# Two transformer layers on one core: read-back copies kept in order on VectorE, query and key splits cut map by map, and another order behind layer 0's last projection

## The chip, the cores and the metric

The kernel runs on one core of a Trainium2 chip. The metric is the device time of one execution in microseconds (us). A page of the profile and the trace come from one further execution, taken by the hardware profiler. The engines are named as there: PE is TensorE, PEld its weight loads, DVE VectorE, ACT ScalarE, POOL GpSimd and SP SyncE, which here mainly issues DMAs. All data in the tables and rows below is fp32 or fp32r, with the tiles named by the program (`Q`, `E`, `M` and so on; a letter behind a `P`, as in `PC`, is a bank of PSUM).

## The reference, cut to what matters

Layer 0 mixes tokens by differential attention, layer 1 by attention over a neighbourhood of the latent grid plus the context. Each is followed by an MLP with a squared ReLU. Shift, scale and gate of every normalization ("modulation") come from a matrix product of a conditioning vector.

```python
D_MODEL, SEQ, CTX_LEN, HEAD_DIM, DEPTH = 1024, 512, 256, 64, 2
DA_HEADS, NA_HEADS, D_FF = 8, 16, 4096

def diff_attend(q, k, v, lam):                 # two maps (m) per head
    s = jnp.einsum('bqhmd,bkhmd->bhmqk', q, k) * ATTN_SCALE
    p = jax.nn.softmax(s, axis=-1)
    w = p[:, :, 0] - lam * p[:, :, 1]
    return jnp.einsum('bhqk,bkhe->bqhe', w, v)

for i in range(DEPTH):
    mod_l = jnp.split(jax.nn.silu(c) @ w_mod[i] + b_mod[i], 6, axis=-1)
    mod_c = jnp.split(jax.nn.silu(c_ctx) @ w_mod[i] + b_mod[i], 6, axis=-1)
    h_l = rms_norm(x, norm1_g[i]) * (1 + mod_l[1]) + mod_l[0]
    h_c = rms_norm(ctx, norm1_g[i]) * (1 + mod_c[1]) + mod_c[0]
    y_l, y_c = mixer[i](h_l, h_c)              # q and k: rms_norm per map, rotary in layer 0
    x = x + mod_l[2] * y_l
    x = x + mod_l[5] * mlp(rms_norm(x, norm2_g[i]) * (1 + mod_l[4]) + mod_l[3])
    # layer 0 does the same for ctx with mod_c
return x
```

Matrix products are needed at fp32 accuracy.

## The kernel before, in words

**Data and stages.** There are 768 tokens: 256 of the context and 512 latent ones, 6 tiles of 128 rows. A product at fp32 accuracy is made of three passes over operands that are each split into a high part (rounded to fp32r) and the remainder, low part (`PASSES`); so most tiles are written twice, the high part by an ACT copy and the low part by a subtraction on DVE. In the profile the stages lie about so: layer 0's first head to 65 us, its heads to 421, its last attention and the projection of heads to 563, its MLP to 1057, layer 1's eight groups of two heads from 1091 to 1403, their projection to 1476, the last MLP to the end.

**The order of the work.** In the attention stages the order is written out by hand in strings that `run()` reads word by word: `START0`, `CYCLE0` for each further head, `TURN0` and `END0` behind the last projection of layer 0's heads, and `START1`, `CYCLE1`, `LAST1`, `END1` for layer 1. A word is a step: Q a half of the projection of one tile to q, k and v; U a turn, which transposes and splits q and k of two tiles (U4 is the turn of tiles 4 and 5); S scores and softmax of one tile; T transposes and splits the softmax of one tile ("turned"); V weighs the values with it; O transposes one tile's output; P half a step of the projection of heads (P0a and P0b are the halves of step 0), x and X fetch and split one head's attention output for it, B begins it; w and c load and split the weights of the next head; m is a visit of the modulation. A prime marks the head before, two primes the one before that. In layer 1 U turns likewise, and N is a piece of a normalization. PE, SP and POOL issue in the written order (`manual_schedule(engines=PINNED)`); for DVE and ACT a scheduler sets the order, except for instructions that are given to `keep_in_program_order`.

**The visits.** The modulation's large product is spread over 40 loads of weights, one for each visit (class `Mods`, l. 1060). A visit runs 8 matmuls with a tile `M` of raw weights (l. 300; rows of the profile that group two visits show x16), adds them up in `MA` (l. 302) and issues the load of the next `M`. From layer 0's second head to the end of its projection there is one buffer for `M`. After the fourth visit of a section the result is stored to DRAM (`rows`). One visit later `rows` is read back into the tile `columns`, turned so that the model dimension lies on the partitions (the DMA is issued on SP). Again a visit later `mod_set` copies `columns` into `mB` (l. 287) or, with the norm's gain, into `mA` (l. 290). The program writes that copy at the visit behind the one that issues the read-back; on DVE the scheduler is free to put it anywhere behind the issue. There are six such copies in the profile.

**A turn.** In layer 0 four transposes (l. 522) put q and k of two tiles into one PSUM bank `C`: the columns 0 to 255 are q, 256 to 511 are k, and the partitions 0 to 63 and 64 to 127 belong to the two maps. `q_split` and `k_split` (l. 450 and 463) write them to SBUF so that each map's scores contract over 128 partitions: q's high part on its own half and the low part on the other and k's high and low parts on both halves each. Their lines are:

| line | engine | what it writes for map m, with a the map's own half and b the other |
|---|---|---|
| 456, 457 | ACT, DVE | layer 0's q: high part in half a, low part in half b |
| 459, 460 | ACT, DVE | the same for layer 1's q, with a gain |
| 467, 469 | ACT | k's high part in a, then in b, both from PSUM |
| 468, 471 | DVE | k's low part in a; for tiles 4 and 5 in b as well, from PSUM |
| 473 | POOL | k's low part in b for the other tiles, from the SBUF half a |

ACT and DVE read the same bank, and the program's waits let them in by turns. Layer 0's turn calls `q_split` first for tiles 0 to 3 and last for tiles 4 and 5 (l. 527 to 531). Layer 1 turns into a bank `A` (transposes l. 664, calls l. 667 to 669); its scores are l. 686, layer 0's are l. 547. Ahead of a turn, a projection (matmuls l. 431) is copied to SBUF (l. 438, ACT), squared there (l. 442, ACT), summed (l. 444, DVE) and scaled (l. 446, DVE), and the low part of the values is written (l. 492, DVE).

**Behind layer 0's last projection.** `TURN0` and `END0` finish the last two heads (weighing l. 582, turned softmax l. 571, output l. 599) and mix in the projection of heads (l. 783, followed by a multiply with the gate at l. 788 and an addition at l. 789, for which the layer's input is fetched by SP). Five visits lie in them.

## Time and profile before

| | |
|---|---|
| median of 3 timed runs | 1846.56 us (1844.48 to 1847.8) |
| profiled execution | 1841.2 us |
| its span | 1839.4 us |
| mean granted clock of PE | 0.977 of full speed |
| PE busy | 1722.8 us, 94% of the span, 9918 matmuls |
| PEld busy | 1519.8 us, 83% |
| DVE busy | 1253.5 us, 68% |
| ACT busy | 937.6 us, 51% |
| POOL busy | 1039.7 us, 57% |
| DMA | 227.29 MB, mean 124 GB/s |

How its rows are read: a row of an instruction has its start, its duration, engine, line, operation, the tiles out and in, and in brackets how long the engine stood idle just before and what ended that wait. A row "a:b" of the windows has the length of the stretch, then for PE, PEld, DVE, ACT and POOL the busy time with the number of instructions, then the mean granted clock of PE, the share of the DMA engines and the GB/s. A row that starts with a line number groups like instructions: busy time and mean ns of one, then the idle time before them by releaser. The line "DMA columns<-rows" is of the list of waits: the idle time that this DMA ended, and the number of times.

### The profile page before, as it was taken

How to read it: one execution, taken by the hardware profiler on the slowest of the kernel's cores; microseconds unless marked ns; L12 is line 12 of the kernel's file. 1: busy time of each engine (PE TensorE's matmuls, PEld its weight loads, DVE VectorE, ACT ScalarE, POOL GpSimd, SP SyncE). 2: the span in 40 equal slices, each digit the busy share in tenths (PEclk: the TensorE clock that was granted, in tenths of full speed). 3: DMA queues.
4: the chain of work that ended last, by engine and by line, in shares of the span. 5: the costliest groups of instructions: out<-in, count | busy, mean ns of one | idle time of the engine just before them, and what ended most of it. 6: DMA issues, size and time to landing. Idle time of an engine off the chain costs nothing.

```text
span 1839.4 us, 27551 instructions
## 1 busy us (share of the span) xinstructions
PE 1722.8 (94%) x9918; PEld 1519.8 (83%) x9918; DVE 1253.5 (68%) x2332; ACT 937.6 (51%) x1962; POOL 1039.7 (57%) x998
## 2 busy tenths in 40 slices
PE   6989999997899999999999999999998889999998
PEld 4878989985688899999997888889887778788877
DVE  4678878886565656464659677778677566676785
ACT  4566767765234343343333456667667254445432
POOL 3755666652334667575767713433355448777774
PEclk9989999998999999999999999999999989999999
DMA  9222221225445545544541334433332434334441
GB/s 335 73 84 78 91 83 64 93 79 190 155 152 165 166 124 146 136 121 100 154 143 58 106 127 130 132 109 118 107 119 96 145 103 138 126 126 138 137 149 46
DMA packets 104809, 227.29 MB, mean 124 GB/s; under 512 B 22160, under 2 KB 38752, under 8 KB 100576
## 3 DMA queue, kind: packets, MB, share of 16 engines
q1 hardware_dynamic: 95152, 212.56, 36.7%
q10 hardware_dynamic: 9520, 12.97, 2.0%
q8 instruction: 78, 1.28, 0.3%
q14 instruction: 59, 0.48, 0.1%
HBM read 207.19 MB, written 18.30 MB: 123 GB/s over the span
## 4 chain that ended last, share of the span: by engine, by line
PE 69%; DVE 12%; ACT 6%; DMA 5%; issue 4%; POOL 4%; ACTq 0%; SPq 0%; POOLq 0%; DVEq 0%
PE PD L875 21%; PE PA L431 14%; PE PA L935 8%; PE PB L935 8%; PE PA L783 3%; PE PA L1016 3%; POOL W L162 2%; PE PS L547 2%; PE PB L582 2%; PE PQ L421 1%; PE PS L686 1%; PE PB L732 1%; PE PB L717 1%; ACT E L553 1%; PE PB L571 1%
## 5 line engine op out<-in xcount | busy, mean ns | idle before, releaser
L162 POOL TENSOR_TENSOR W<-R,W 128x512 fp32r<-128x512 f32 x214 | 328.5, 1561 | 143.4 <-ACT W L156 142.0
L875 PE MATMUL PD<-Q,W 128*128 128x384 f32 (+2 forms) x1992 | 381.5, 345 | 7.2 <-DVE Q L352 6.0
L875 PEld LDWEIGHTS PD<-Q,W 128*128 128x128 f32 x1992 | 348.1, 190 | 30.2 <-DVE Q L352 7.3
L156 ACT ACTIVATE W<-R 128x1024 fp32r<-128x1024 f32 (+1 forms) x137 | 138.7, 1014 | 138.5 <-POOL W L162 34.9
L162 POOL TENSOR_TENSOR W<-N,W 128x512 fp32r<-128x512 f32 x98 | 141.8, 1469 | 114.7 <-ACT W L156 95.3
L935 PE MATMUL PA<-W,H 128*128 128x512 f32 x732 | 191.2, 396 | 6.5 <-DVE Q L943 3.1
L935 PE MATMUL PB<-W,H 128*128 128x512 f32 x738 | 191.2, 394 | 3.2 <-DVE Q L943 2.0
L431 PE MATMUL PA<-W,Q 128*128 128x384 f32 (+1 forms) x1008 | 175.2, 326 | 0.0
L935 PEld LDWEIGHTS PA<-W,H 128*128 128x128 f32 x732 | 138.9, 191 | 36.1 <-issue 3.5
L935 PEld LDWEIGHTS PB<-W,H 128*128 128x128 f32 x738 | 139.4, 190 | 32.9 <-DVE Q L943 2.7
L431 PEld LDWEIGHTS PA<-W,Q 128*128 128x128 f32 x1008 | 159.4, 192 | 1.0 <-ACT H L469 0.2
L312 POOL TENSOR_TENSOR SQ<-SQ,half 128x4 f32<-128x4 f32 (+1 forms) x96 | 94.0, 980 | 109.6 <-DVE SQ L444 108.2
L431 PE MATMUL PA<-WB,H 128*128 128x384 f32 x576 | 110.0, 343 | 4.8 <-DVE Q L492 4.8
L156 ACT ACTIVATE W<-N 128x1024 fp32r<-128x1024 f32 x49 | 51.8, 1058 | 113.4 <-PE PB L935 36.8
L431 PEld LDWEIGHTS PA<-WB,H 128*128 128x128 f32 x576 | 99.9, 190 | 6.2 <-DVE Q L492 3.9
L783 PE MATMUL PA<-W,H 128*128 128x512 f32 x384 | 98.5, 408 | 6.0 <-DVE T L788 5.3
L875 PE MATMUL PD<-H,W 128*128 128x512 f32 (+1 forms) x408 | 95.2, 382 | 0.2 <-DVE H L352 0.2
L783 PEld LDWEIGHTS PA<-W,H 128*128 128x128 f32 x384 | 72.7, 195 | 25.3 <-DVE T L788 6.4
L698 POOL TENSOR_SCALAR E<-E,SA 128x256 f32<-128x256 f32 x64 | 59.1, 935 | 58.4 <-DVE SA L695 58.1
L875 PEld LDWEIGHTS PD<-H,W 128*128 128x128 f32 x408 | 75.0, 192 | 15.7 <-DVE H L352 0.9
L893 DVE SCALAR_TENSOR_TENSOR H<-N,H 128x512 fp32r<-128x512 f32 (+1 forms) x57 | 59.5, 1055 | 35.4 <-ACT H L892 35.2
L431 PE MATMUL PA<-WA,H 128*128 128x384 f32 x432 | 83.2, 344 | 0.0
(292 smaller groups left out, 3619.0 us busy)
## 6 DMA issues: line engine op xcount, KB each, us to landing
R<-in_w_dram SPq DMA_DIRECT2D x93, 512.0 KB
M<-in_wmod_dram SPq DMA_DIRECT2D x32, 1024.0 KB
N<-in_w_dram SPq DMA_DIRECT2D x49, 512.0 KB
R<-in_wqa_dram SPq DMA_DIRECT2D x32, 384.0 KB
R<-in_wqb_dram SPq DMA_DIRECT2D x32, 384.0 KB
C<-in_wmod_dram SPq DMA_DIRECT2D x16, 512.0 KB
M<-in_wmod_dram SPq DMA_DIRECT2D x16, 512.0 KB
C<-in_w_dram SPq DMA_DIRECT2D x14, 512.0 KB
```

Source lines behind the costliest of these rows:

```text
L156: high = nc.scalar.activation(w[:, 0, :n], raw, AF.Copy)
L162: low = (eng or nc.gpsimd).tensor_sub(w[:, 1, o:e], raw[:, o:e], w[:, 0, o:e].bitcast(F32))
L312: nc.gpsimd.tensor_tensor(r, ss, self.half[:, :n], op=ALU.pow)
L431: nc.tensor.matmul(acc[:, :n], hT[kt][:, x, P * i:P * i + P], w[kt // 2][:, y, o:o + n], start=(kt == 0 and p == 0), stop=(kt == KT - 1 an ...
L547: nc.tensor.matmul(s[:, c0:c1], q[:, m, P * i:P * i + P], k[:, m, c0:c1], start=p == 0, stop=p == 1)
L582: nc.tensor.matmul(po[:, :256], wT[:, x, P * kt:P * kt + P], v[:, kt].rearrange("p a d -> p (a d)"), start=(x, kt) == jobs[0], stop=(x, kt ...
L698: nc.gpsimd.tensor_scalar_mul(e[:, 1, o:o + 256], e[:, 1, o:o + 256], r[:, 1:2])
L783: nc.tensor.matmul(ps, oHL[h][:, x, c:c + P], w[h // 2][:, y, 512 * (h % 2):512 * (h % 2) + 512], start=(first and h == hs[0] and p == 0), ...
L875: nc.tensor.matmul(ps[:, at:at + b1 - b0], w[kt // 4][:, x, o:o + P], hT[kt][:, y, b0:b1], start=(kt == 0 and p == 0), stop=(kt == KT - 1 ...
L893: nc.vector.scalar_tensor_tensor(u[:, 1], src, 1.0, u[:, 0].bitcast(F32), op0=ALU.mult, op1=ALU.subtract)
L935: nc.tensor.matmul(ps, u[:, x, f, P * i:P * i + P], w[:, y, 512 * f:512 * f + 512], start=(f == 0 and p == 0), stop=(f == 1 and p == 2))
L1016: nc.tensor.matmul(ps, hd[:, x, P * i - c0:P * i - c0 + P], w[f][:, y, 512 * n:512 * n + 512], start=(f == 0 and p == 0), stop=(f == len(h ...
```

## The change

It has three parts.

1. `mod_set` returns its instruction, and `visit` gives it to `keep_in_program_order`, so that the copy of `columns` stands on DVE where the program writes it.
2. `q_split` and `k_split` become one function `qk_split`, which goes map by map: k's high part, k's low part, then their second copies, then q. The second copy of the high part (on ACT) and of the low part (DVE for tiles 4 and 5, POOL for the others) are read from the first copy in SBUF; POOL's were so before.
3. `TURN0` and `END0` have another order: O2'', O3'', V4'' and the turn U4' stand ahead of S1' and T0'; some weighings (V) stand ahead of the next tile's turned softmax (T); the visit at the end of `TURN0` stands behind V1', and the last visit stands between P5a and P5b. There are five visits as before.

```diff
-TURN0 = """x0 x1 x2 x3 S1' O2'' O3'' V4'' T0' U4' X0 V5'' T1' X1 m"""
-END0 = """S2' O4'' V0' O5'' S3' X2 x4 V1' O0' T2' X3 m P0a S4' T3' V2' x5 X4 P1a S5' T4' V3' O1' X5 B0 P0b
-T5' V4' x6 P1b O2' O3' m V5' P2a P2b O4' P3a m P3b O5' P4a X6 P4b m P5a P5b"""
+TURN0 = """x0 x1 x2 x3 O2'' O3'' V4'' U4' S1' T0' X0 V5'' X1 T1'"""
+END0 = """S2' O4'' V0' O5'' S3' X2 x4 V1' m O0' T2' X3 P0a S4' V2' x5 X4 O1' T3' P1a S5' V3' T4' X5 B0 P0b V4' x6
+T5' P1b O2' V5' m O3' P2a P2b O4' P3a m P3b O5' P4a X6 P4b m P5a m P5b"""
...
         if sec % 3 == 0:
-            self.nc.vector.tensor_copy(self.mB[:, l, norm, ks, :], t)
-        else:
-            n = ks.stop - ks.start
-            self.nc.vector.scalar_tensor_tensor(
+            return self.nc.vector.tensor_copy(self.mB[:, l, norm, ks, :], t)
+        n = ks.stop - ks.start
+        return self.nc.vector.scalar_tensor_tensor(
...
-    def q_split(self, ps, q, cols, gain=None):
+    def qk_split(self, pq, q, qc, pk, kh, kl, kc, soon, gain=None):
         nc = self.nc
         lo, hi = slice(0, 64), slice(64, 128)
         for m, (a, b) in enumerate(((lo, hi), (hi, lo))):
+            nc.scalar.activation(kh[a, m, kc], pk[a], AF.Copy)
+            nc.vector.tensor_sub(kl[a, m, kc], pk[a], kh[a, m, kc].bitcast(F32))
+            nc.scalar.activation(kh[b, m, kc], kh[a, m, kc].bitcast(F32), AF.Copy)
+            (nc.vector if soon else nc.gpsimd).tensor_copy(kl[b, m, kc], kl[a, m, kc].bitcast(F32))
+            if pq is None:
+                continue
             if gain is None:
-                nc.scalar.activation(q[a, m, cols], ps[a], AF.Copy)
-                nc.vector.tensor_sub(q[b, m, cols], ps[a], q[a, m, cols].bitcast(F32))
+                nc.scalar.activation(q[a, m, qc], pq[a], AF.Copy)
+                nc.vector.tensor_sub(q[b, m, qc], pq[a], q[a, m, qc].bitcast(F32))
...
-    def k_split(self, ps, kh, kl, cols, soon):
...
-        for m, (a, b) in enumerate(((lo, hi), (hi, lo))):
-            nc.scalar.activation(kh[a, m, cols], ps[a], AF.Copy)
-            nc.vector.tensor_sub(kl[a, m, cols], ps[a], kh[a, m, cols].bitcast(F32))
-            nc.scalar.activation(kh[b, m, cols], ps[a], AF.Copy)
-            if soon:
-                nc.vector.tensor_sub(kl[b, m, cols], ps[a], kh[a, m, cols].bitcast(F32))
-            else:
-                nc.gpsimd.tensor_copy(kl[b, m, cols], kl[a, m, cols].bitcast(F32))
...
             cols = slice(P * i, P * i + 256)
-            if i < 4:
-                self.q_split(ps[:, 0:256], q, cols)
-            self.k_split(ps[:, 256:512], kh, kl, cols, i == 4)
-            if i == 4:
-                self.q_split(ps[:, 0:256], q, cols)
+            self.qk_split(ps[:, 0:256], q, cols, ps[:, 256:512], kh, kl, cols, i == 4)
...
         if self.landed:
-            b.mod_set(*self.landed, slice(0, KT), b.columns)
+            b.tc.keep_in_program_order(b.mod_set(*self.landed, slice(0, KT), b.columns))
```

Layer 1's turn calls `qk_split` in the same way, with the gain, and without q for the two context tiles.

The order on DVE around the first read-back of layer 0 before: L287 is the copy of `columns`; L591 scales an output tile, L559 combines the two maps of a softmax, L457 is the low part of q in a turn.

```order
L556 RECIPROCAL SA_3373<-SA_3357 128x2
L558 TENSOR_SCALAR SA_3375<-SA_3373,SA_3357,neglam 128x1
L287 COPY mB<-columns 128x16
L591 SCALAR_TENSOR_TENSOR O_3328<-O_3324,SO_3331,one 128x128
L559 SCALAR_TENSOR_TENSOR E_3356<-E_3356,SA_3375 128x768
L457 TENSOR_TENSOR Q_3158<-PC_3391,Q_3158 64x256
```

And the same copy on DVE now; L301 is the accumulation into `MA` of the next visit (l. 302 before), L462 the low part of q or k in a turn, L484 the low part of the values, L443 a sum of squares.

```order
L305 TENSOR_SCALAR SO_4108<-SO_4108 128x1
L484 TENSOR_TENSOR Q_3640<-PA_4079,Q_3640 128x128
L287 COPY mB<-columns 128x16
L462 TENSOR_TENSOR Q_3835<-PC_4062,Q_3835 64x256
L301 TENSOR_TENSOR MA_3352<-PA_4143,MA_3352 128x256
L443 TENSOR_REDUCE SQ_4130<-sq_83 128x4
```

The copy moved a whole head further down the queue, to just ahead of the accumulation of the visit at which the program writes it.

The order on PE in `TURN0` before, from the end of the scores S1' on: L547 scores, L599 output, L582 weighing, L571 turned softmax, L522 the transposes of the turn U4', L300 a visit.

```order
L547 MATMUL PS_5546<-Q_5184,Q_5182 128x256
L599 MATMUL PB_5563<-ident,O_5348 128x128
L599 MATMUL PB_5566<-ident,O_5452 128x128
L582 MATMUL PB_5570<-Q_4310,X_5392 128x256 x12
L571 MATMUL PB_5594<-ident,E_5498 128x128 x2
L522 MATMUL PC_5599<-ident,Y_5316 128x128 x2
L522 MATMUL PC_5599<-ident,Y_5470 128x128 x2
L582 MATMUL PB_5620<-Q_4310,X_5516 128x256 x12
L571 MATMUL PB_5644<-ident,E_5544 128x128 x2
L300 MATMUL PA_5653<-M_5496,silu 32x256 x8
```

The same on PE now; the lines are those of the changed file (L587 output, L570 weighing, L514 transposes of the turn, L535 scores, L559 turned softmax).

```order
L587 MATMUL PB_5545<-ident,O_5348 128x128
L587 MATMUL PB_5548<-ident,O_5452 128x128
L570 MATMUL PB_5552<-Q_4310,X_5392 128x256 x12
L514 MATMUL PC_5575<-ident,Y_5316 128x128 x2
L514 MATMUL PC_5575<-ident,Y_5470 128x128 x2
L535 MATMUL PS_5594<-Q_5183,Q_5182 128x256
L535 MATMUL PS_5594<-Q_5184,Q_5182 128x256
L535 MATMUL PS_5594<-Q_5183,Q_5182 128x256
L535 MATMUL PS_5594<-Q_5184,Q_5182 128x256
L559 MATMUL PB_5611<-ident,E_5498 128x128 x2
L570 MATMUL PB_5620<-Q_4310,X_5516 128x256 x12
L559 MATMUL PB_5648<-ident,E_5592 128x128 x2
```

The turn U4' now comes ahead of the scores S1' and of the first turned softmax, and no visit follows T1'.

The order on PE around the last visits before, from the end of P4b to the start of the last steps (L783 projection of heads, L300 a visit):

```order
L783 MATMUL PA_6138<-W_5054,H_5948 128x512 x3
L300 MATMUL PA_6165<-M_6118,silu 32x256 x8
L783 MATMUL PA_6183<-W_4954,H_5616 128x512 x3
L783 MATMUL PA_6183<-W_4954,H_5649 128x512 x3
L783 MATMUL PA_6183<-W_5000,H_5745 128x512 x3
L783 MATMUL PA_6183<-W_5000,H_5782 128x512 x3
L783 MATMUL PA_6183<-W_5054,H_5869 128x512 x3
L783 MATMUL PA_6183<-W_5054,H_5948 128x512 x3
L783 MATMUL PA_6235<-W_5953,H_6148 128x512 x3
```

And now (L770 projection, L299 a visit):

```order
L770 MATMUL PA_6126<-W_5054,H_5936 128x512 x3
L299 MATMUL PA_6153<-M_6106,silu 32x256 x8
L770 MATMUL PA_6165<-W_4954,H_5616 128x512 x3
L770 MATMUL PA_6165<-W_4954,H_5643 128x512 x3
L770 MATMUL PA_6165<-W_5000,H_5727 128x512 x3
L299 MATMUL PA_6175<-M_6163,silu 32x256 x8
L770 MATMUL PA_6165<-W_5000,H_5782 128x512 x3
L770 MATMUL PA_6165<-W_5054,H_5844 128x512 x3
L770 MATMUL PA_6165<-W_5054,H_5936 128x512 x3
L770 MATMUL PA_6235<-W_5941,H_6136 128x512 x3
```

A second visit, with a tile `M` of its own load, now stands behind the first nine matmuls of step 5.

More of the change, by code (lines that the diff above doesn't have):

```diff
@@ L286, in mod_set @@
         if sec % 3 == 0:
[L287 to L292 removed]
+            return self.nc.vector.tensor_copy(self.mB[:, l, norm, ks, :], t)
+        n = ks.stop - ks.start
+        return self.nc.vector.scalar_tensor_tensor(
+            self.mA[:, l, norm, ks, :], t, 1.0, self.gT[:, norm, l, ks, None].to_broadcast([P, n, 2]),
+            op0=ALU.add, op1=ALU.mult)
     def mod_visit(self, acc, v, raws, bank):
@@ L666, in turn @@
                 nc.tensor.transpose(ps[:, P * j:P * j + P], f[:, 0:P], self.ident)
-            if i0:
-                self.q_split(ps[:, 256:512], q, slice(P * i0 - 256, P * i0), gain=self.gqk)
-            self.k_split(ps[:, :256], kh, kl, slice(P * i0, P * i0 + 256), i0 == 4)
+            self.qk_split(ps[:, 256:512] if i0 else None, q, slice(P * i0 - 256, P * i0),
+                          ps[:, :256], kh, kl, slice(P * i0, P * i0 + 256), i0 == 4, self.gqk)
             if i0 == 4:
```

8 lines of the change are left out of this document (2 added, 6 removed).

## The prediction

> **What bounds the kernel now.** I read the page first, then the waits of the tile `columns`, the timeline around them, and the windows from one repeated place of a head to the next.
>
> ```profile
> span 1839.4 us, 27551 instructions
> PE 1722.8 (94%) x9918; PEld 1519.8 (83%) x9918; DVE 1253.5 (68%) x2332; ACT 937.6 (51%) x1962; POOL 1039.7 (57%) x998
> PE 69%; DVE 12%; ACT 6%; DMA 5%; issue 4%; POOL 4%; ACTq 0%; SPq 0%; POOLq 0%; DVEq 0%
> ```
>
> The profiled execution took 1841.2 us, 1.8 more than its span; the three timed runs have their median at 1846.56, 5.4 above it. TensorE is busy 94% of the span and holds 69% of the chain that ended last. An edit pays only where it takes away a wait of TensorE, or the slow clock that follows one. The first place is the read-back of the modulation columns:
>
> ```profile
>   DMA columns<-rows: 12.0, 6
> 271.60 0.18 DVE L287 COPY mB<-columns 128x16 f32<-128x16 f32 x1 [3.67 <-DMA columns<-rows]
> 368.88 0.17 DVE L290 SCALAR_TENSOR_TENSOR mA<-columns,gT 128x16 f32<-128x16 f32 x1 [3.30 <-DMA columns<-rows]
> 321.98 0.43 DVE L302 TENSOR_TENSOR MA<-PA,MA 128x256 f32<-128x256 f32 x1
> 273.11 0.52 PE L571 MATMUL PB<-ident,E 128*128 128x128 f32 x3 [1.08 <-DVE E L559]
> 275.06 3.75 PE L431 MATMUL PA<-WB,H 128*128 128x384 f32 x12 [0.65 <-DVE Q L492]
> 372.35 2.36 PE L431 MATMUL PA<-WB,H 128*128 128x384 f32 x12 [0.65 <-DVE Q L492]
> 275.00:279.00 4.00, 3.94 (x14) 3.66 (x14) 3.68 (x11) 3.19 (x11) 1.96 (x4) 0.61 0.61 248
> 231.30:282.46 51.16, 48.59 (x321) 44.38 (x319) 39.85 (x94) 34.37 (x98) 31.27 (x42) 0.97 0.27 83
> 282.46:328.95 46.49, 46.26 (x321) 43.02 (x320) 39.48 (x93) 34.39 (x99) 31.31 (x42) 1.00 0.26 89
> 328.95:379.75 50.80, 47.42 (x320) 42.98 (x319) 39.65 (x92) 34.38 (x96) 31.27 (x42) 1.00 0.28 89
> ```
>
> VectorE runs its queue in order. At 271.60 and 368.88 it stood still for 3.67 and 3.30 us in front of an instruction of 128x16 elements, because the DMA had not landed. Softmax work was queued behind, so TensorE waited (1.08 and 0.65 us are named) and lost its clock: 12 matmuls took 3.75 us where the same 12 took 2.36 elsewhere, at a mean granted clock of 0.61. The last three rows are three successive heads of layer 0, cut where the turn of tiles 4 and 5 (U4') transposes. The work is the same (321, 321 and 320 matmuls, VectorE busy alike), but the heads with a read-back last 51.16 and 50.80 us and the one without 46.49. In layer 1, cut where U2 of one group ends its head, heads alternate between two forms, and the last two of the slow form hold a read-back:
>
> ```profile
> 1150.27:1191.17 40.90, 38.70 (x293) 36.24 (x292) 30.80 (x73) 29.01 (x72) 17.53 (x24) 1.00 0.34 113
> 1191.17:1230.25 39.08, 38.54 (x292) 36.25 (x291) 30.65 (x72) 28.06 (x70) 14.91 (x21) 1.00 0.39 129
> 1230.25:1274.16 43.91, 39.92 (x293) 37.46 (x291) 31.05 (x74) 29.13 (x72) 17.32 (x24) 0.96 0.35 106
> 1313.23:1357.86 44.63, 41.27 (x292) 38.82 (x291) 31.21 (x74) 29.00 (x72) 17.25 (x24) 0.92 0.32 95
> 1234.54 0.47 PE L664 MATMUL PA<-ident,Y 128*128 128x128 f32 x1 [3.91 <-DVE Y L446]
> 1316.88 0.47 PE L664 MATMUL PA<-ident,Y 128*128 128x128 f32 x1 [3.27 <-DVE Y L446]
> ```
>
> Slow form without a read-back 40.90, with one 43.91 and 44.63; the other form 39.08. TensorE waits 3.91 and 3.27 us there for VectorE's L446, queued behind the copy. The second place lies behind layer 0's last projection of heads, where the new order is:
>
> ```profile
> 421.43:480.39 58.96, 41.74 (x241) 32.82 (x241) 39.66 (x87) 30.16 (x81) 16.55 (x20) 0.86 0.51 180
> 424.04 0.74 PE L547 MATMUL PS<-Q,Q 128*128 128x256 f32 x4 [2.60 <-ACT E L553]
> 428.41 0.60 PE L522 MATMUL PC<-ident,Y 128*128 128x128 f32 x4
> 435.28 2.90 PE L547 MATMUL PL<-Q,Q 128*128 128x512 f32 x8 [3.24 <-DVE Q L457]
> 445.01 0.30 PE L599 MATMUL PB<-ident,O 128*128 128x128 f32 x1 [2.40 <-DVE O L591]
> 472.40 2.71 PE L582 MATMUL PB<-Q,X 128*128 128x256 f32 x12 [3.11 <-DVE X L574]
> ```
>
> TensorE worked 41.74 of these 58.96 us at a mean clock of 0.86: 17.2 us of waits, and 0.14 x 58.96 = 8.3 us of clock.
>
> **The change, part by part.** *Read-back copies.* Pinned to program order, each copy stands in the next visit's place. For the first one that is just ahead of the accumulation into `MA` which ran at 321.98, 50 us behind the landing at 271.60, so it waits for nothing. What was queued behind it runs where VectorE had stood still. Layer 0: 51.16 - 46.49 = 4.67 and 50.80 - 46.49 = 4.31. Layer 1: 43.91 - 40.90 = 3.01 and 44.63 - 40.90 = 3.73. Together 15.7. The other two read-backs lie in the MLP and behind the projection; the 12.0 us of idle leave them 12.0 - 3.67 - 3.30 = 5.0 less what layer 1 has of it; I take nothing, since VectorE there is not what matmuls wait for. I take 15 of the 15.7. Bounds: all of it and a little of the others, 16; and half, 8, if another wait stands close behind.
>
> *Turns.* Both engines read one PSUM bank in a turn, and the program makes them take turns at it:
>
> ```profile
> 433.84 0.42 DVE L457 TENSOR_TENSOR Q<-PC,Q 64x256 fp32r<-64x256 f32 x1 [0.44 <-ACT Q L456]
> 434.29 0.38 ACT L456 ACTIVATE Q<-PC 64x256 fp32r<-64x256 f32 x1 [0.48 <-DVE Q L457]
> L471 DVE TENSOR_TENSOR Q<-PC,Q 64x256 fp32r<-64x256 f32 x16 | 6.8, 422 | 0.8 <-ACT Q L469 0.4
> L351 DVE CAST H<-Y 128x256 fp32r<-128x256 f32 x8 | 2.2, 284 | 0.0
> L438 ACT ACTIVATE Y<-PA 128x256 f32<-128x256 f32 x74 | 28.2, 382 | 20.2 <-PE PA L431 17.7 <-PE PC L522 1.6
> L442 ACT ACTIVATE sq<-Y 128x256 f32<-128x256 f32 x80 | 33.5, 418 | 3.0 <-DVE SQ L444 2.7
> 1118.20 0.39 PE L686 MATMUL PS<-H,H 128*128 128x256 f32 x1 [0.78 <-DVE H L471]
> 1366.26 0.84 PE L686 MATMUL PS<-H,H 128*128 128x256 f32 x2 [1.23 <-ACT H L469]
> ```
>
> One handover is 434.29 - 433.84 = 0.45 us. Before, a turn that scores wait for (tiles 4 and 5) has 12 such steps, in the others 10; now 8, since the second copies read SBUF, and map 0 is complete after four. That brings the scores' operands some 4 x 0.45 = 1.8 us forward. The copy on VectorE in place of the subtraction costs 0.28 (nearest row L351, twice the partitions) for 0.42. The second copy on ScalarE reads SBUF: L442, from SBUF, is 0.04 slower than L438, from PSUM, and it waits for ScalarE's own first copy, which no row prices. Most turns are covered: the head of 46.49 us has 0.23 idle. Paid back are the waits of L686 for the splits, 0.78 + 1.23 = 2.0, and, as an estimate, 0.3 in each of the three heads of layer 1's slow form, since the copies of k on GpSimd come free sooner for the power behind them: 3.0 gained. Bounds: a gain of 6, if three quarters of the slow form's excess (3 x 1.82 = 5.5) go besides the 2.0; a loss of 4, if 0.04 shows on TensorE at each of 48 turns x 2 copies.
>
> [...]
>
> *Order.* Three effects, from the diff and the order of TensorE. (a) U4' stands ahead of S1' and T0'. Its transposes began at 428.41 and S2' at 435.28, after waiting 3.24 for the split. Moved forward by S1' (0.74) and the 2.60 that S1' waited, less about 1.0 that O2'' then waits for the banks that T5'' holds, with a shorter split, S2' could start 4 us earlier. But T1', now directly in front of S2', needs the softmax of S1':
>
> ```profile
> 427.78 0.48 DVE L559 SCALAR_TENSOR_TENSOR E<-E,SA 128x256 f32<-128x256 f32 x1
> 494.30 1.07 PE L300 MATMUL PA<-M,silu 128*32 128x256 f32 x16
> 495.84 7.09 PE L783 MATMUL PA<-W,H 128*128 128x512 f32 x30 [0.46 <-DVE T L788]
> L300 PEldq EVENT_SEMAPHORE  x2: 51/51/51, 483.8 to 493.6; - x2
> 487.92 0.33 SPq L173 DMA_DIRECT2D M<-in_wmod_dram  x1
> 494.30 0.69 DVE L789 TENSOR_TENSOR Q<-Q,T 128x512 f32<-128x512 f32 x1 [2.74 <-DMA Q<-in_xin_dram]
> ```
>
> That softmax ended at 428.26, 4.2 us after S1' began; S1', T0' and V5'' cover some 2.9, and VectorE has the split's work in between. I take a gain of 2.7 for S2' (bounds 0 and 5). (b) A visit (1.07) leaves the path ahead of P0a and fills part of the 2.40 in front of O0': 1.07 gained. The weighing of one tile now stands ahead of the turning of the next, so it no longer waits for a bank that this turning holds; of the waits there I take the 3.11 away and leave the rest: 3.0. With about 7 of 17.2 us of waits gone, the clock's 8.3 falls by the same share, 3.3; TensorE works 71% of the time: 2.3. Front together: 9.1 gained. (c) The last two visits now have only P5a between them, 9 matmuls x 7.09 / 30 = 2.1 us. They use one buffer `M`. A load of it was issued at 487.92, and TensorE's sequencer was released at 493.6: 5.7 us. The load starts when the first visit is done, so the second waits 5.7 - 2.1 = 3.6. Then P5b's x rides behind the next `M` load: VectorE waited 2.74 for such a one until 494.30, 6.4 us after that load's issue. P5b and the two tiles that free banks allow, 9 + 12 matmuls, cover 5.0: about 1.5 more with the multiply behind. The visit itself adds 1.07, a slow clock behind the wait 1.0. Tail: 7.2 lost. Order: 9.1 - 7.2 = 1.9, taken as 2 gained; bounds a gain of 10 (the tail's waits hidden) and a loss of 6 (the front gives 1).
>
> Sum: 15 + 3 + 2 = 20 us. From 1841.2 the profiled execution goes to 1821.2, the median from 1846.56 to **1826.6**.
>
> **The rivals.** (1) *Another wait takes the read-back's place.* For: the slow form of layer 1 waits for L446 without a read-back too. Against: in layer 0 the head without one has 0.23 us idle. At half, 8 for 15, the time is 1833.6. (2) *The tail eats the order.* The order loses 6 where I gain 2: the second visit waits out the whole load and little of the front comes through. It speaks for it that one buffer is sure; 1834.6. (3) *All of it comes.* Order 10, turns 6, read-backs 15: 31 gained, 1815.6. (4) *Slower: the second copies stretch every turn.* Each waits until ScalarE has written the first, and the copy on VectorE likewise. With x us a copy on TensorE's path at 48 turns x 2, it decides from 20 / 96 = 0.21 us on; at 0.3 the loss is 28.8, the time 1826.6 + 28.8 = 1855.4. Against: the idle of 0.23 a head shows that turns are covered. (5) *The clock does not fall in short waits.* Then a read-back is worth only TensorE's idle in the windows: (2.57 - 0.23) + (3.38 - 0.23) + (3.99 - 2.20) + (3.36 - 2.20) = 8.4, and the time 1833.2. The granted 0.61 behind waits of 1.08 and 0.65 speaks against it. [...] That the copies are not moved at all is excluded by the order.
>
> **How the numbers follow.** My forecast, 1820 to 1833, has 0.62; (1) 0.13, (2) 0.10, (3) 0.08, (4) 0.04, (5) 0.03. A measurement of this kernel tells about 0.2% from no change, 3.7 us. Faster by more: the forecast, (3), (5), and most of (1) and (2), 0.90. Within: the lower ends of (1) and (2), where they come together, 0.06. Slower: (4), 0.04. The bounds (7 up for read-backs and turns each, 8 for the order; 1, 3 and 8 down), set against each other as roots of squares, give 1826.6 + 12.7 and - 9; with (3) and without the farthest of (1) and (2) the range is 1814 to 1838.
>
> **What would show it.** Right: the copies from `columns` wait under 0.3 us; heads of layer 0 all last about 46.5 us, those of layer 1 no more than 41; the window behind the projection has a clock above 0.86; the second of the last two visits waits 3 to 4 us for `M`. Wrong: heads with a read-back still near 50 (1); L547 and L686 wait longer for the splits (4); the stretch of 58.96 us is still above 56 (2), or below 46 (3), where I expect some 50.

## The result, and the profile after

The changed kernel takes 1818.93 us (median of 4 runs, 1815.85 to 1822.82) against 1845.52 of the kernel before in the same comparison (4 runs, 1841.4 to 1847.8). The ratio is 0.9864 with a 95% interval of 0.9847 to 0.9881, that is 25.1 us less (22.0 to 28.2). A second comparison, in another set of runs, gave 0.9872 (0.9857 to 0.9886). The profiled execution took 1815.85 us. The forecast was 1826.6, with a range of 1814 to 1838: the time lies inside it, just below the 1820 to 1833 that was given most of the chance. The gain is a quarter larger than the 20 us of the sum, and its terms came out otherwise than they were written. Of the page:

```profile
span 1814.1 us, 27553 instructions
PE 1710.1 (94%) x9918; PEld 1509.4 (83%) x9918; DVE 1247.6 (69%) x2332; ACT 941.6 (52%) x1962; POOL 1040.7 (57%) x998
PE 67%; DVE 12%; ACT 6%; POOL 6%; issue 5%; DMA 3%; ACTq 0%; POOLq 0%; DVEq 0%; SPq 0%
```

The work is the same. TensorE is busy 12.7 us less, and its time at half clock fell from 85.3 to 54.7 us (mean granted clock 0.977 and 0.985); the rest of the 25.3 us of span is idle time that went. The first pinned copy on VectorE, in the timeline of the changed kernel (L301 is the accumulation of the next visit):

```profile
316.06 0.29 DVE L484 TENSOR_TENSOR Q<-PA,Q 128x128 fp32r<-128x128 f32 x1 [0.40 <-ACT Q L483]
316.26 0.17 DVE L287 COPY mB<-columns 128x16 f32<-128x16 f32 x1
316.46 0.42 DVE L462 TENSOR_TENSOR Q<-PC,Q 64x256 fp32r<-64x256 f32 x1
316.92 0.42 DVE L301 TENSOR_TENSOR MA<-PA,MA 128x256 f32<-128x256 f32 x1
```

No bracket stands at the copy: it waits for nothing, and the DMA is no longer in the list of waits. The windows of the same heads of layer 0, of four groups of layer 1, and of the stretch behind layer 0's last projection (from the same matmul to the same matmul as the 58.96 us of before):

```profile
228.73:276.74 48.01, 46.72 (x320) 42.93 (x319) 38.31 (x93) 34.93 (x98) 31.77 (x42) 1.00 0.28 89
276.74:323.74 47.00, 46.43 (x320) 42.93 (x319) 38.39 (x94) 34.71 (x98) 31.84 (x42) 1.00 0.26 88
323.74:371.92 48.18, 46.75 (x321) 42.97 (x320) 38.28 (x91) 35.05 (x97) 31.81 (x42) 1.00 0.29 94
413.28:462.91 49.63, 36.12 (x225) 28.72 (x226) 39.73 (x87) 29.28 (x80) 17.50 (x18) 0.93 0.52 192
1176.70:1215.40 38.70, 38.33 (x293) 36.29 (x292) 29.70 (x71) 28.40 (x71) 15.29 (x21) 1.00 0.37 125
1215.40:1256.30 40.90, 38.72 (x293) 36.25 (x292) 31.58 (x75) 28.55 (x71) 16.75 (x25) 1.00 0.40 118
1256.30:1294.90 38.60, 38.23 (x292) 36.20 (x290) 29.65 (x71) 28.32 (x71) 15.21 (x21) 1.00 0.38 125
1294.90:1337.30 42.40, 40.20 (x292) 37.73 (x291) 31.63 (x75) 28.53 (x71) 16.73 (x25) 0.96 0.33 99
```

The heads with a read-back are 3.2 and 2.6 us shorter, not 4.7 and 4.3, and the one without is 0.5 longer. One of the four groups of layer 1 shown still lasts over 41 us (42.40). The stretch behind the projection went from 58.96 to 49.63, where 50 was expected; its clock rose from 0.86 to 0.93. It holds 225 matmul records and not 241, because one visit now stands behind it: a visit has 16 records in the profile (in the one of before the 40 visits have 640 at L300, for 8 matmuls each), so rows with x16 are one visit and not two. What follows it on TensorE is the tail with the last two visits:

```profile
483.05 1.07 PE L299 MATMUL PA<-M,silu 128*32 128x256 f32 x16 [2.87 <-DMA M<-in_wmod_dram]
484.06 5.08 PE L770 MATMUL PA<-W,H 128*128 128x512 f32 x21
492.18 2.08 PE L770 MATMUL PA<-W,H 128*128 128x512 f32 x4 [3.05 <-DVE T L775]
```

The visit waits 2.87 us for its load of `M`, and the matmuls behind the first 21 of the last steps then 3.05 for VectorE. SP and VectorE show why: the fetch of the last step's input was issued directly behind the next load of `M` (484.18), and VectorE's addition (L776) waited for it.

```profile
484.18 0.33 SPq L173 DMA_DIRECT2D M<-in_wmod_dram  x1
484.56 0.42 SPq L795 DMA_DIRECT2D Q<-in_xin_dram  x1
```

```profile
489.98 1.35 DVE L776 TENSOR_TENSOR Q<-Q,T 128x512 f32<-128x512 f32 x1 [2.84 <-DMA Q<-in_xin_dram]
```

To see where the time went, each matmul of the changed kernel was set against the same matmul of before. The table holds the median of (start now - start before) in slices of 20 us, at selected places; the other columns are the experiments below. Negative is earlier. The column "again" is a second trace of the changed kernel. It differs from the first by 1.4 to 3.4 us in these rows, though VectorE and ScalarE run the same instructions in the same order in both; so differences of this size between two columns can be chance (last section), and steps that come again in several columns weigh more.

```
before at   changed  again  pin only  split only  order only  no read-back  old order  visit moved
  60 us       0.0    2.0      1.6       -1.3         2.7          3.6          -0.1        2.8
 200         -3.0   -1.6     -0.3       -3.7         2.1          2.8          -2.6       -0.7
 260         -2.4   -1.0     -0.3       -3.1         2.0          2.8          -2.0       -0.1
 280         -5.8   -4.3     -3.9       -3.7         2.0         -0.8          -5.3       -3.5
 360         -5.0   -3.6     -3.4       -2.8         2.0         -0.8          -4.6       -2.7
 380         -8.2   -6.8     -6.6       -2.4         2.4         -4.0          -7.8       -6.0
 400         -8.2   -6.8     -6.6       -2.4         2.3         -4.0          -7.8       -6.0
 480        -17.5  -15.5     -6.0       -4.4        -4.2         -4.1         -10.0      -14.9
 520        -12.6   -9.2     -8.3       -6.0         3.5         -4.3         -12.3      -15.9
1060        -14.1  -11.1     -9.7       -7.5         3.7         -4.3         -13.7      -14.6
1220        -14.9  -11.7     -9.8       -5.2         5.4         -4.2         -13.6      -16.8
1240        -18.2  -15.0    -11.3       -4.9         7.1         -5.7         -15.4      -20.1
1300        -18.3  -15.2    -11.3       -5.0         7.1         -5.7         -15.5      -20.2
1320        -20.8  -19.2    -15.0       -6.5         6.1         -9.4         -19.5      -24.2
1400        -24.4  -22.7    -15.5      -10.1         6.0        -10.5         -22.9      -28.2
1820        -25.3  -22.4    -13.0       -9.2         5.8         -7.2         -21.9      -28.9
```

### The profile page after: what moved, and what is told of

Same layout as the page of the kernel before. It is cut to its first block, busy times and chain, and to the rows that moved or that the text cites. A ratio compares the mean times of both kernels' runs of the same rounds, so it can differ in the third digit from the quotient of the medians.

```text
span 1814.1 us, 27553 instructions
## 1 busy us (share of the span) xinstructions
PE 1710.1 (94%) x9918; PEld 1509.4 (83%) x9918; DVE 1247.6 (69%) x2332; ACT 941.6 (52%) x1962; POOL 1040.7 (57%) x998
## 4 chain that ended last, share of the span: by engine, by line
PE 67%; DVE 12%; ACT 6%; POOL 6%; issue 5%; DMA 3%; ACTq 0%; POOLq 0%; DVEq 0%; SPq 0%
PE PD L862 20%; PE PA L430 14%; PE PB L922 7%; PE PA L922 7%; POOL W L162 4%; PE PA L770 3%; PE PA L1003 3%; PE PS L535 2%; PE PB L570 1%; PE PQ L420 1%; PE PB L719 1%; ACT E L541 1%; PE PS L673 1%; PE PA L299 1%; PE PB L704 1%
## 5 line engine op out<-in xcount | busy, mean ns | idle before, releaser
L770 PE MATMUL PA<-W,H 128*128 128x512 f32 x384 | 96.6, 403 | 7.0 <-DVE T L775 5.6
L770 PEld LDWEIGHTS PA<-W,H 128*128 128x128 f32 x384 | 71.5, 192 | 24.7 <-DVE T L775 6.6
```

The costliest lines, as they stand in the source:

```text
L770: nc.tensor.matmul(ps, oHL[h][:, x, c:c + P], w[h // 2][:, y, 512 * (h % 2):512 * (h % 2) + 512], start=(first and h == hs[0] and p == 0), ...
```

## The experiments

The theory was the prediction's: 15 us from the copies, 3 from the split in layer 1, 2 from the order, each by the mechanism written there. Three kernels change the one before by one part alone (only the copies, only the split, only the order); the others ask for the reason of what these showed.

**Only the copies kept in order.** The edit is part 1 of the change alone; besides `mod_set` returning its instruction it is this line:

```diff
-            b.mod_set(*self.landed, slice(0, KT), b.columns)
+            b.tc.keep_in_program_order(b.mod_set(*self.landed, slice(0, KT), b.columns))
```

> The kernel before, with the copies of the read-back tile `columns` kept in program order on VectorE and nothing else changed. Theory (the prediction's term): TensorE was held up by the copies that waited for the DMA, so 15 us go; the heads of layer 0 with a read-back fall from 51.2 and 50.8 us to 46.5, and the waits of VectorE for `columns` from 12.0 us to none. Rival 1 (the trace of the changed kernel, laid beside that of before, shows steps of only 3.3, 3.1, 3.3 and 2.5 us at the four places): about 12 us. Rival 2 (another wait takes the place): 8 us or less, with the heads at 49. Rival 3 (the clock does not fall in short waits): 8.4 us, with the granted clock of those windows as before.

Measured: 1831.7 us (6 runs), ratio 0.9938 (0.992 to 0.9956), 11.4 us less (8.1 to 14.7). The steps in the table at the four places are 3.6, 3.2, 1.5 and 3.7, and a fifth of 2.3 us lies at 504 us. Rival 1's 12 us is what came. The theory's 15 lies just outside the interval and rival 2's 8 at its edge; rival 3's 8.4 is not excluded by the time, but the granted clock of the first head with a read-back rose from 0.97 to 1.00. The heads in the windows of this kernel:

```profile
231.00:278.60 47.60, 46.55 (x321) 42.96 (x320) 39.87 (x93) 34.29 (x98) 31.26 (x42) 1.00 0.28 89
278.60:325.60 47.00, 46.27 (x320) 42.93 (x319) 39.82 (x94) 34.41 (x99) 31.24 (x42) 1.00 0.27 88
325.60:373.20 47.60, 46.52 (x320) 42.92 (x319) 39.58 (x91) 34.39 (x96) 31.27 (x42) 1.00 0.31 95
```

They fall to 47.6, not to 46.5, and the head in between, which now holds a copy, rises to 47.0. The half microsecond comes as one wait, 4 us behind the copy; there the scheduler also put a few instructions of VectorE and ScalarE in another order, and whether the copy's 0.17 us or that order costs it is not shown.

**No read-back at all.** The DMAs to `columns` are left out and a constant stands in it, so the modulation of the later norms is not the reference's. With nothing to wait for, the scheduler put all six copies at the start (1.5 to 7.7 us); the order of VectorE's other instructions stayed as before. So this kernel shows the heads with neither the read-back nor the copy.

```diff
+        nc.vector.memset(self.columns, 0.01)
...
-        if self.fetched:
-            for s in range(2):
-                nc.sync.dma_start(b.columns[:, :, s], b.rows[(*self.fetched, s)].rearrange("(k p) -> p k", p=P))
```

> The kernel before without any read-back: the DMAs from `rows` to `columns` are left out and `columns` is filled with a constant once, so that the second layer's and the MLPs' modulation has wrong numbers; the copies stay, and wait for nothing. It is the most that any placing of the copies can bring. Theory: as the kernel with the copies kept in order, within 2 us, 15 us faster than before; the heads of layer 0 all last 46.5. Rival 1: the alternate heads of layer 0 still differ by 1 us, as in the changed kernel (48.0 and 48.2 against 47.0), which would put that difference down to something else than the read-back. Rival 2: it is faster than the pinned copies by 3 us or more, so that something of the read-back is left when its copies are pinned.

Measured: 1830.07 us, ratio 0.9937 (0.9918 to 0.9957), as with the pinned copies. The difference of the two times is uncertain by 5 us, but the steps in the table at the four places are the same 3.6, 3.2, 1.5 and 3.7, so pinning leaves nothing of the wait there, and rival 2 falls. Rival 1 holds:

```profile
234.10:281.70 47.60, 46.56 (x321) 42.96 (x320) 39.91 (x93) 34.29 (x98) 31.26 (x42) 1.00 0.26 89
281.70:328.20 46.50, 46.29 (x321) 43.03 (x320) 39.46 (x94) 34.41 (x99) 31.29 (x42) 1.00 0.26 89
328.20:375.70 47.50, 46.71 (x320) 42.86 (x319) 39.17 (x91) 34.28 (x96) 31.26 (x42) 1.00 0.26 95
```

The two heads that had a read-back are 1.1 and 1.0 us longer than the one between even without it. The head of 46.49 us that the prediction took as the measure of "the same work" is not the same.

**Stores on another queue.** Those heads also hold the four stores of a finished section, which ScalarE issues (in the changed kernel's timeline of ScalarE):

```profile
259.70 1.16 ACTq L1079 DMA_DIRECT2D rows<-MA  x4
261.67 0.90 ACT L541 ACTIVATE E<-PS,SA 128x768 f32<-128x768 f32 x1 [1.90 <-DVE SA L540]
```

The experiment starts from the kernel with the moved visit (below):

```diff
-                    nc.scalar.dma_start(b.rows[l, sec, :, 256 * q:256 * q + 256], acc[32 * q:32 * q + 2])
+                    nc.sync.dma_start(b.rows[l, sec, :, 256 * q:256 * q + 256], acc[32 * q:32 * q + 2])
```

> The kernel with the moved visit (the last visit stands behind V2' and x5, otherwise as the changed kernel), and the four stores of a finished section of the modulation issued on SP in place of ScalarE's queue. It asks what makes the heads of layer 0 with a read-back 1 us longer when the copies no longer wait (48.0 and 48.2 against 47.0), since they were 1.1 longer without any read-back too. Theory: it is the four stores, which take 1.15 us of ScalarE's queue in just these heads (259.70 to 260.86 us); then these heads come down to 47.0 to 47.3, the groups of layer 1 with a store gain as well, and the time falls by 2 to 5 us against the kernel with the moved visit. Rival 1: it is something else in these heads; then they stay at 48 and the time within 1 us. Rival 2: on SP the stores wait for the accumulation and hold up the weights queued behind; then TensorE waits for DMAs and it is slower.

Measured: 1808.41 us, ratio 0.9797 (0.9776 to 0.9818) against 0.9825 (0.9809 to 0.9841) of the kernel it starts from, on another chip: 2.5 us less by the medians, and by the two ratios 5 us (0.3 to 10). The windows are clearer:

```profile
227.30:274.40 47.10, 46.48 (x321) 43.03 (x320) 38.41 (x93) 34.72 (x99) 31.88 (x42) 1.00 0.29 91
274.40:321.50 47.10, 46.49 (x321) 43.03 (x320) 38.43 (x94) 34.70 (x99) 31.83 (x42) 1.00 0.26 88
321.50:369.50 48.00, 46.68 (x320) 42.94 (x319) 38.48 (x91) 34.69 (x95) 31.90 (x42) 1.00 0.30 94
```

The first of the long heads comes down to 47.1, as the theory has it. The second stays at 48.0. Behind the stores it changes as the first does: in the changed kernel TensorE waits 0.40 and 0.63 us there in the first head and 0.46 and 0.70 in the second, and now none and 0.34, and none and 0.35. But a wait of 0.71 us (at 337.46, for VectorE's L547) stands ahead of them, where the changed kernel has none, and why is not shown. So the waits behind the stores went in both heads; the theory holds for the length of the first alone. The scheduler also put some instructions of both engines in another order behind the stores' old place, which this run cannot separate from the stores themselves.

**Only the split.** The functions `qk_split` and its calls alone.

> The kernel before, with the split of q and k map by map and the second copies read from SBUF, and nothing else changed. Theory (the prediction's term): 3 us faster, all of it in layer 1. Rival 1 (the steps of the changed kernel's trace that lie at no read-back: some 3.5 us between 80 and 200 us, some 0.6 in every group of layer 1 and 3 behind it): 6 to 8 us faster. Rival 2 (the second copies from SBUF stretch turns): no gain or slower, with TensorE's waits at the turns longer than before.

Measured: 1831.13 us, ratio 0.9938 (0.992 to 0.9956), 11.4 us less (8.1 to 14.7). Rival 2 falls, and the theory's 3 us with it; even rival 1's 8 lies at the edge of the interval.

**The split's order without the copies from SBUF.** From `qk_split` two sources are set back to PSUM:

```diff
-            nc.scalar.activation(kh[b, m, kc], kh[a, m, kc].bitcast(F32), AF.Copy)
-            (nc.vector if soon else nc.gpsimd).tensor_copy(kl[b, m, kc], kl[a, m, kc].bitcast(F32))
+            nc.scalar.activation(kh[b, m, kc], pk[a], AF.Copy)
+            if soon:
+                nc.vector.tensor_sub(kl[b, m, kc], pk[a], kh[a, m, kc].bitcast(F32))
+            else:
+                nc.gpsimd.tensor_copy(kl[b, m, kc], kl[a, m, kc].bitcast(F32))
```

> The kernel before with k and q split map by map, k first, as in the changed kernel, but with the second copies read from PSUM as before: the order of the split alone, without its copies from SBUF. The split with copies from SBUF alone was 11.4 us faster than before. Theory (the prediction's reason): the gain comes from the handovers of the bank that the copies from SBUF save, so this kernel gains less than half, 0 to 5 us. Rival 1: it comes from the order, k ahead of q and one map after the other; then it gains 9 us or more. Rival 2: copies from SBUF cost ScalarE 0.04 us each on the path; then it is faster than the one with copies from SBUF, by up to 4 us.

Measured: 1836.82 us, ratio 0.9969 (0.9955 to 0.9982), 5.7 us less (3.3 to 8.3): by the medians half of the split's gain is the order of the split and half the source (for the source 5.7 us, from 1.6 to 9.9). So the reason of the theory, the handovers that the copies save, accounts for about half; rival 1's 9 and rival 2 are out. Groups of ScalarE's second copies, by form, first of this kernel, then of the one with the split as changed:

```profile
L457 ACT ACTIVATE Q<-PC 64x256 fp32r<-64x256 f32 x48 | 18.2, 379 | 14.9 <-DVE Q L456 14.2
L457 ACT ACTIVATE H<-PA 64x256 fp32r<-64x256 f32 x48 | 18.1, 377 | 12.7 <-DVE H L456 11.8
```

```profile
L457 ACT ACTIVATE H<-H 64x256 fp32r<-64x256 f32 x48 | 20.1, 418 | 1.4
L457 ACT ACTIVATE Q<-Q 64x256 fp32r<-64x256 f32 x48 | 20.0, 418 | 1.3
```

From SBUF a copy is 0.04 us longer, but ScalarE's idle time before it falls from 27.6 to 2.7 us in 96 copies, because it need not wait its turn at the bank. Selected rows of a turn of tiles 4 and 5 with the changed split, the start of map 0 and the end of map 1, show it:

```profile
425.38 1.06 PE L515 MATMUL PC<-ident,Y 128*128 128x128 f32 x4
426.48 0.38 ACT L455 ACTIVATE Q<-PC 64x256 fp32r<-64x256 f32 x1
426.89 0.42 ACT L457 ACTIVATE Q<-Q 64x256 fp32r<-64x256 f32 x1
426.89 0.42 DVE L456 TENSOR_TENSOR Q<-PC,Q 64x256 fp32r<-64x256 f32 x1
427.34 0.38 ACT L462 ACTIVATE Q<-PC 64x256 fp32r<-64x256 f32 x1
430.90 0.43 DVE L463 TENSOR_TENSOR Q<-PC,Q 64x256 fp32r<-64x256 f32 x1
431.47 0.47 PE L536 MATMUL PL<-Q,Q 128*128 128x512 f32 x1 [1.94 <-DVE Q L463]
```

At 426.89 both engines start at once, where they took turns before (VectorE at 433.84, ScalarE at 434.29 us). From the transposes to the scores it is 431.47 - 425.38 = 6.1 us; before it was 435.28 - 428.41 = 6.9.

**The split in one layer only.** `qk_split` is called in layer 1 alone, then in layer 0 alone; the other layer keeps the old functions.

> The kernel before with the new split of q and k in layer 1 only; layer 0 splits as before. In both layers it was 11.4 us faster. Theory of the prediction: layer 1 holds all of the gain, so 11 us here. Rival (the trace with the new split in both layers: 4 us less between 1100 and 1400 us, the rest in layer 0's first heads and behind its last projection): 4 us here.

> The kernel before with the new split of q and k in layer 0 only; layer 1 splits as before. Theory of the prediction: nothing, since layer 0's turns are covered. Rival: 5 to 7 us faster, of it some 2.7 in the first heads (80 to 200 us) and 3.5 behind the last projection, with up to 1.6 given back in the covered heads between (0.3 us each).

Measured: layer 1 alone 1837.33 us, ratio 0.9973 (0.9954 to 0.9993), 5.0 us less (1.3 to 8.5); layer 0 alone 1836.51 us, ratio 0.9957 (0.994 to 0.9974), 7.9 us less (4.8 to 11.1). So the theory, by which layer 0 gains nothing, falls; by these values layer 1, the prediction's place, holds less than half. Layer 0's part lies in the first heads, which the windows from the first turn of head 0 to the first turn of head 3 show (before, then with the split alone):

```profile
73.00:200.80 127.80, 113.31 (x740) 102.42 (x739) 101.06 (x242) 84.49 (x244) 78.44 (x106) 0.96 0.24 80
```

```profile
71.70:196.60 124.90, 112.44 (x740) 100.87 (x739) 99.98 (x243) 85.79 (x244) 79.01 (x105) 0.97 0.24 82
```

2.9 us go there, 14.5 us of waits against 12.5, and some 3.6 behind the last projection (table, from 400 to 520 us). The trace with the split in layer 0 alone has the same 2.9 in the first heads but only 1.4 behind the projection, and places 4 us more in the last MLP, where nothing was changed; so of the 7.9 the traces place 4 to 6.5 in layer 0.

**Only the order.** `TURN0` and `END0` alone.

> The kernel before, with the new TURN0 and END0 and nothing else changed. Theory (the prediction's term): 9 us gained ahead of the last two visits and 7 lost at them, 2 us faster in all. Rival 1 (the changed kernel's trace: 9.3 gained and 4.9 lost): 4.4 us faster. Rival 2: the front's gain needs the shorter turn as well, since U4' stands ahead of S1' there; then the order alone gains less than 5 ahead of the visits and the kernel is no faster, or slower by up to 3.

Measured: 1843.57 us (12 runs), ratio 1.0008 (0.9995 to 1.0021): 1.5 us slower, from 0.9 faster to 3.9 slower. The gains of the theory and of rival 1 are out. The time is rival 2's, but not by its reason: in the table the kernel gains 6.5 us from 400 to 480, more than rival 2's 5, and loses 7.7 from there to 520; its tail:

```profile
496.31 1.07 PE L300 MATMUL PA<-M,silu 128*32 128x256 f32 x16 [2.80 <-DMA M<-in_wmod_dram]
507.34 2.92 PE L783 MATMUL PA<-W,H 128*128 128x512 f32 x6 [4.97 <-DVE T L788]
```

**The changed kernel with the old order, and once more itself.** The first is the change without its third part.

> The changed kernel with TURN0 and END0 as before: the copies kept in order and the split map by map from SBUF, without the new order. Theory (the prediction's term): 2 us slower than the changed kernel. Rival 1 (the order alone measured 1.5 us slower, and the three parts add up): 1 to 2 us faster than the changed kernel, 22.8 us faster than before. Rival 2: the new order gains by the shorter split and by the copy that no longer stands in its tail, and is worth 4 us beside them; then it is 4 us slower than the changed kernel.

> The changed kernel itself once more, on the chip of the other three, so that they can be set against it: 25.1 us faster than before was measured (21.8 to 28.2). All theories expect 22 to 28.

Measured on one chip: 1817.17 us (1815.36 to 1819.28, ratio 0.9857, 0.9841 to 0.9873) with the old order, 1819.31 (1817.5 to 1821.01, ratio 0.9872, 0.9857 to 0.9886) for the changed kernel. By the medians the new order costs 2.1 us beside the other two parts, as rival 1 has it, though against before the kernel gains 26.3 us (23.4 to 29.3) and not that rival's 22.8; the two ratios set against each other leave 0.0015 +- 0.0022, from 1.2 us gained to 6.8 lost, so that it gains 2 is out of the interval, and 4 far out; that it costs anything is not shown by either comparison. The second trace of the changed kernel has the same waits in the tail, with a slower TensorE besides (the visit took 1.93 us for 1.07, the 21 matmuls behind it 7.03 for 5.08):

```profile
485.04 1.93 PE L299 MATMUL PA<-M,silu 128*32 128x256 f32 x16 [2.82 <-DMA M<-in_wmod_dram]
486.90 7.03 PE L770 MATMUL PA<-W,H 128*128 128x512 f32 x21
496.22 5.99 PE L770 MATMUL PA<-W,H 128*128 128x512 f32 x23 [2.29 <-DVE T L775]
```

**The last visit moved.** From the changed kernel:

```diff
-... S4' V2' x5 X4 O1' T3' P1a ... P4b m P5a m P5b
+... S4' V2' x5 m X4 O1' T3' P1a ... P4b m P5a P5b
```

> The changed kernel with one of its five visits moved: the one between P5a and P5b now stands behind V2' and the fetch of x5, some 40 us ahead. Theory (the prediction's term for the tail): the second visit waits for its load of `M` and the last step's addition for the fetch queued behind that load, so moving it away takes back what the changed kernel's trace loses there against before, 4.9 us: 4 to 5 us faster than the changed kernel. Rival 1: the visit that is moved ahead holds up the softmax chain there, or waits for its own load, and takes 2 or more of it back. Rival 2: the tail's loss is not of the visits; then nothing changes, within 1 us.

Measured on the same chip: 1810.89 us (1807.52 to 1813.06), ratio 0.9825 (0.9809 to 0.9841), 8.4 us less than the changed kernel by the medians (4.6 to 12.7 by the ratios) and 6.3 less than with the old order. The tail on TensorE:

```profile
479.79 1.07 PE L299 MATMUL PA<-M,silu 128*32 128x256 f32 x16 [0.30 <-DMA M<-in_wmod_dram]
481.94 7.09 PE L770 MATMUL PA<-W,H 128*128 128x512 f32 x30 [1.07 <-DVE T L775]
489.25 4.11 PE L770 MATMUL PA<-W,H 128*128 128x512 f32 x14 [0.22 <-DVE T L775]
```

The waits of 2.87 and 3.05 are now 0.30 and 1.07, and where the visit went it costs nothing that can be told (from 400 to 480 us this kernel gains 8.9, the changed one 9.3 and 8.7 in its two traces). From 480 to 520 it gains 1.0 where the changed kernel loses 4.9, and 6.3 in its second trace. So the theory has the place and the reason right and the size low: 5.9 and 7.3 us by the traces for its 4 to 5. This kernel and the one with the stores on SP are faster than both kernels of the case.

## Why the prediction was right or wrong

The three parts, each measured alone, add up to 11.4 + 11.4 - 1.5 = 21.3 us, and together they gave 25.1 (22.0 to 28.2) and 23.6 (21.0 to 26.3) in two comparisons. They add up, within what was measured. That the forecast's sum of 20 came near is partly luck: its term for the split was 8.4 us too low, and those for the read-backs and the order together 7 too high.

*Read-backs: right mechanism, 15 forecast, 11.4 measured.* The failed step is "The work is the same" of the heads: the 4.67 and 4.31 hold 1.1 and 1.0 us that are there without any read-back. Where they were found the steps are 3.6 and 3.2. With the pinned copy the head in which it now stands is 0.5 longer, which the sum did not have. Against that, "I take nothing" for the other two was wrong too: at 504 us the copy waited only 0.47 us and took 0.70, but it stood before the gate's multiply, and waits of TensorE (0.46, 0.27, 1.00 and 1.03 at L783) went with it, 2.3 us by the table. In layer 1 the sum 3.0 + 3.7 came out as 1.5 + 3.7. At the first of these places 2.12 of the 3.91 us for which TensorE waited for L446 stay with the pinned copies, and the same 2.12 without any read-back; the step of 1.5 is no more than the 3.91 - 2.12 = 1.79 that went of the wait, so what the clock cost there stays in both, by this estimate. In the changed kernel the wait is 1.81, the granted clock of the group is 1.00 where it was 0.96 before, and the step is near the forecast's size (3.3).

*Split: 3 forecast, 11.4 measured, beyond its bound of 6.* The failed step is "Most turns are covered". It was read from one head of 46.49 us in the middle of layer 0, and there it is so: those heads gain nothing from the split, and lose up to 0.4 (the column "split only" goes up from -3.7 to -2.4 between 200 and 400 us). The turns in layer 0's first heads and behind its last projection are not covered, and the split in layer 0 alone measured 7.9 us, of which the traces place 4 to 6.5 there; layer 1 alone measured 5.0. In layer 1 the waits of L686 (2.6 us before) are 0.2 now, as was forecast:

```profile
L673 PE MATMUL PS<-H,H 128*128 128x256 f32 x256 | 36.8, 286 | 0.2 <-ACT E L680 0.2
```

The second copies' price was taken rightly at 0.04 (418 against 379 ns); the loss of 4 that was the bound for it did not come, since the wait at the bank was the larger cost (27.6 us of ScalarE's idle time ahead of 96 copies from PSUM, 2.7 from SBUF).

*Order: 2 gained forecast, 1.5 to 2.1 lost by the medians, neither clear of nothing.* The halves look right: 9.1 forecast for the front, 9.3 and 8.7 in the two traces; 7.2 for the tail, 4.9 and 6.3 there. The front's number is partly luck. Of its 17.2 us of waits about 7 were to go, and 49.63 - 36.12 = 13.5 are left, so 3.7 went; of the 8.3 us of clock 3.3 were to go, and 0.07 x 49.63 = 3.5 are left, so 4.8 went. And both sums were made against the kernel before. The kernel with the old order has 2.2 of the front's gain by the split and gains another 2.3 in the tail by the pinned copy, which the new order's wait for `M` hides; so of the front about 7 belong to the order, and in the tail it costs 7 to 9. The failed step is the setting off: what two parts gain in the same place was counted for one of them. The start of that stage in the changed kernel, T1' and then S2':

```profile
423.21 0.53 PE L559 MATMUL PB<-ident,E 128*128 128x128 f32 x2 [3.47 <-DVE E L547]
425.09 2.50 PE L535 MATMUL PL<-Q,Q 128*128 128x512 f32 x6 [1.35 <-DVE Q L462]
```

T1' does wait for the softmax of S1', as was foreseen, and S2' then for its split. S2' came 435.28 - 425.09 = 10.2 us earlier, 2.0 beyond the 8.2 that had been gained before it, where 2.7 was taken; the visit's wait for `M` is 2.87 for 3.6, and the one behind it 3.05 for 1.5.

*The rivals.* Nothing took the read-back's place (1). The tail did eat the order's gain (2), but with about half of the 8 us of that rival, and the front came through. The copies from SBUF did not stretch turns (4); they gained. The clock (5) fell behind the first read-back and not behind the second (0.97 and 1.00 in these heads), although TensorE's idle time was larger there (3.38 us for 2.57); how it was spread is told below.

## What to carry to other kernels

To price a wait, compare stretches that hold the same instructions on every queue, not only the same matmuls: here four stores on ScalarE's queue were about a fifth of a supposed wait in one head (0.9 of 4.67 us). Whether an operation is covered is a matter of the stage, so ask for it in each, above all at the start and the end of a pipeline. Where two edits act at one place, count the gain for one of them only, and look at what is queued behind a load on its queue before a step that needs it (here TensorE waited 3.05 us behind a fetch that was issued after the load of `M`).

## What the runs showed of the hardware

The stretches at half clock lay on a grid. In each of the 13 traces every stretch at a granted clock of 0.5 begins on one grid of 3.413 us and lasts one or several of its steps (the end of the run cuts the last one); the grid's place differs from run to run. Before has 17 such stretches, of 3.41 to 13.65 us, and the changed kernel 11, of 3.41 to 10.24; those of before at 127.94 and 274.71 us, for one, begin 146.77 / 3.4133 = 43.0 steps apart. The traces were laid on that grid and TensorE's busy share in each full-clock step ("window" here) was compared with the clock of the next (behind the first 18 us):

```
busy share of the window   windows   followed by half clock
below 0.43                     132           132
0.43 to 0.58                   115            43
above 0.58                    6336             2
```

The borders 0.43 and 0.58 were chosen from these counts, and the ends of matmuls are modelled, so they are rough. Before and the changed kernel alone have 23 windows below 0.43, all followed by half clock, 17 between, of which 5 were, and 977 above, of which none was. Before, the read-back at 271 us fell into one window (busy 0.52, the longest wait named there 1.08 us), and 3.41 us at half clock followed; the longer idle time at 369 us was split over two (0.71 and 0.66), and the clock stayed at 1.00. One fall of a single step more or less is worth an estimated 3.41 / 2 = 1.7 us, which may be the chance steps noted above the table; that was not tried.
